# Bias tables made on 128 partitions, paddings filled by GpSimd, and lo parts on VectorE in the second block

## The chip, the cores and the metric

The kernel runs on one core of one Trainium2 chip. The metric is the device time of one execution in microseconds, the median of several runs. In the profile the engines are PE (TensorE matmul), PEld (TensorE weight load), DVE (VectorE), ACT (ScalarE), POOL (GpSimd) and SP (SyncE, which only issues DMAs here). L12 is line 12 of the kernel before.

## The reference

Two transformer blocks run one after the other on 512 tokens of width 1024, in float32. The first has a mixing layer, in which one input projection is split over four mixers, and a feed-forward layer:

```python
z = rms_norm(x, norm1_g) @ w_in
z_pool, s_b, s_c, s_h, c_a, c_g, zq, zk, zv = jnp.split(z, idx, axis=-1)
y_pool = pool_mixer(z_pool, pool_w, pool_scale)          # running sums over 2, 4, 8, 16 tokens
y_sconv = s_b * causal_dwconv(s_c * s_h, sconv_w)        # 3 taps
u = causal_dwconv(c_a * jax.nn.sigmoid(c_g), conf_dw_w) + conf_dw_b   # 31 taps
y_conf = jax.nn.silu(layer_norm(u, conf_ln_g, conf_ln_b))
y_attn = diff_attention(q, k, v, ..., rel_bias)
x = x + jnp.concatenate([y_pool, y_sconv, y_conf, y_attn], axis=-1) @ w_out
x = x + (jax.nn.silu(h2 @ w_gate) * (h2 @ w_up)) @ w_down
```

Both the attention here and the one in the second block add a bias that depends only on the distance of query and key (`rel_bias[rel_bucket(dist)]`, 32 buckets, 4 and 8 heads). The second block prepends 16 meta tokens, so that 528 positions count. Its first half (`layer_ab`) is an attention over the 128 best keys of each query, which an indexer scores and a top-k selects, beside a gated linear attention; its second half (`layer_cd`) is a retention beside a stick-breaking attention.

## The kernel before

**Matrix products.** Activations lie with the features on the partitions. Each float32 factor is split into a hi part (rounded) and a lo part (the rest), and each product is three TensorE products: hi by hi, hi by lo, lo by hi (`f_acc`, L144; `t_proj`, L163). Weights come in blocks of 128 x 1024 values. For each block `weights` issues one load on SP's queue into `wraw` (two buffers, L119), then for each half ScalarE makes the hi part (`whi`, L129) and the engine `self.lo` makes the lo part (`wlo`, L130), with four buffers each. `self.lo` is VectorE, but in `layer_ab` it is GpSimd until the top-k selection is through, and VectorE again from there.

**Order.** Each engine works through its queue in order. A compiler puts the queues together ahead of the run, by priorities: `self.chain()` stands highest, `self.first()` (weights and evictions) next, and the rest by its place in the code. It places an instruction where it reckons that its inputs and its tile's memory are there.

**Setup.** `tables` makes the two bias tables, L378 and L382: a product of the bias (32 buckets by heads) with a one-hot matrix (32 by 640 and by 656 columns). The result lies on 4 and on 8 partitions. VectorE brings it to SBUF (L379, which adds the mask row for future keys, and L383). Two DMAs on GpSimd's queue (L384, L385) write it to DRAM with 32 copies of each row, so that `sheared` (L393) can load each partition with its own shift. The meta tokens' eight loads follow (L387). The tiles of this step lie in a pool of their own, `setup`, which ends with the function.

**First block, mixing layer (`layer1`).** The pool `l1` is opened after `setup`, and part of it lies on the same memory. Its tiles are made in the order qT, kT, cs, B1 (the first table, loaded by GpSimd's queue), pw, u. The projections run in the order cg, ca (`fproj`, evicted at L418), then v, k, q by token (`t_proj`), then z, sc, sh, sb. u = ca * sigmoid(cg) is formed at L446 with 30 columns of zeros ahead (L437). The convolution over 31 taps is 2 x 31 operations of VectorE on u (L560, L562), of normal priority. Attention runs in the background, some steps of it after each few products (`logits` L492 to L503, `turn`, `values` L522, `finish`). The pooling sums (L579, L591, L592) read z with 16 columns of zeros ahead (L567); GpSimd subtracts (L593) and TensorE multiplies with pw (L604). The short convolution reads sc with two columns of zeros ahead (L572), with GpSimd's products at L594 and L600. `mix` splits each mixer's output in hi and lo (L102, L103). The output projection comes in two parts: `add_out(mixed[:4])` for pooling and short convolution, then `add_out(mixed[4:])` for the long convolution, once it is normalised (L613 to L632), and attention.

**Second block, first half (`layer_ab`).** The indexer's scores are products into two PSUM banks, then ScalarE's Relu (L817) and VectorE's weighted sum (L814, L818). The top-k is 16 rounds of VectorE's MAX8 (L827) and MATCH_REPLACE8 (L828) for each of four query tiles. During it TensorE makes the next projections, whose weights come through L129 and L130.

Of the kernel before, what the change touches and what calls it, by code (L numbers as in the profile page):

```python
# [8 lines left out]
F32 = mybir.dt.float32  # L9
# [4 lines left out]
OP = mybir.AluOpType  # L14
# [4 lines left out]
S = 512  # L19
# [5 lines left out]
NEG = -1e30  # L25
# [7 lines left out]
COPIES = 32  # L33
# [20 lines left out]
N1 = 640  # L54
N2 = 656


class Kern:
# [303 lines left out]
    def tables(self):  # L362

        nc, io = self.nc, self.io
        self.tab1 = self.dram.tile([4, COPIES, N1], F32, name="tab1")
        self.tab2 = self.dram.tile([8, COPIES, N2], F32, name="tab2")
        with self.tc.tile_pool(name="setup", bufs=1) as p:
            oh = p.tile([32, N1 + N2], F32, name="oh")
            nc.sync.dma_start(oh, io["onehot"])
            mrow = p.tile([4, N1], F32, name="mrow")  # L370
            nc.sync.dma_start(mrow, io["mrow"])
            rb = p.tile([32, 12], F32, name="relb")
            nc.sync.dma_start(rb, io["relb"])
            t1 = p.tile([4, N1], F32, name="t1")
            t2 = p.tile([8, N2], F32, name="t2")
            for c0, c1 in ((0, 512), (512, N1)):
                ps = self.ch("a")
                nc.tensor.matmul(ps[:4, :c1 - c0], lhsT=rb[:, 0:4], rhs=oh[:, c0:c1], start=True, stop=True)  # L378
                nc.vector.tensor_tensor(out=t1[:, c0:c1], in0=ps[:4, :c1 - c0], in1=mrow[:, c0:c1], op=OP.add)  # L379
            for c0, c1 in ((0, 512), (512, N2)):  # L380
                ps = self.ch("a")
                nc.tensor.matmul(ps[:8, :c1 - c0], lhsT=rb[:, 4:12], rhs=oh[:, N1 + c0:N1 + c1], start=True, stop=True)  # L382
                nc.vector.tensor_copy(t2[:, c0:c1], ps[:8, :c1 - c0])  # L383
            nc.gpsimd.dma_start(self.tab1, t1[:, None, :].to_broadcast([4, COPIES, N1]))  # L384
            nc.gpsimd.dma_start(self.tab2, t2[:, None, :].to_broadcast([8, COPIES, N2]))  # L385
            for k in range(KT):
                nc.gpsimd.dma_start(self.x[k][:, 0:M], io["meta"][k])  # L387

# [7 lines left out]
    def layer1(self):  # L396
        nc, tc = self.nc, self.tc
# [6 lines left out]
        rc, rb = self.norm(acc, False)  # L404
        rbx = rb[:, M:T]
        self.tables()
        with tc.tile_pool(name="l1", bufs=1, reuse_waits="tile") as p:
# [4 lines left out]
            def fproj(out):  # L412
                for f in range(2):
                    w = self.weights(8, 128)
                    ps = self.mm()
                    self.f_acc([ps], w, 0, 128, act, X)
                    with self.first():
                        nc.vector.tensor_tensor(out=out[:, f], in0=ps, in1=rbx, op=OP.mult)  # L418


            qT, kT = (p.tile([128, 8, S], F32R, name=n) for n in ("qT", "kT"))
            cs = p.tile([128, NCS1], F32, name="cs1")
            nc.gpsimd.dma_start(cs, self.io["cs1"])
            B1 = p.tile([128, 4, S], F32, name="B1")
# [7 lines left out]
            lam, gq, gs = self.lam, self.gq, self.gs  # L432


            PADC = 30
            u = p.tile([128, 2, PADC + S], F32, name="u")
            nc.vector.memset(u[:, :, :PADC], 0.0)  # L437
            ca, cg = X2(S), X2(S)
            fproj(cg)
            with self.chain():  # L440
# [3 lines left out]
            with self.chain():  # L444
                for f in range(2):
                    nc.vector.tensor_tensor(out=u[:, f, PADC:], in0=ca[:, f], in1=cg[:, f], op=OP.mult)  # L446

# [116 lines left out]

            PADP = 16
            z = G(PADP + S, "z", "ktok")
            nc.vector.memset(z[:, :, :PADP], 0.0)  # L567
# [4 lines left out]
            nc.vector.memset(sc[:, :, :PADS], 0.0)  # L572
            fproj(sc[:, :, PADS:])
            fproj(sh)
            fproj(sb)
# [26 lines left out]
            for f in range(2):  # L602
                ps = self.ch("b")
# [6 lines left out]
            with self.chain():  # L610
                ps = self.ch("b")
# [6 lines left out]
                ps = self.ch("b")  # L618
# [5 lines left out]
                ps = self.ch("b")  # L624
# [149 lines left out]
    def layer_ab(self, act, acc):  # L774
        nc, tc = self.nc, self.tc
        rc, rb = self.norm(acc, True)
        self.nqk = 12
        self.lo = nc.gpsimd
        with tc.tile_pool(name="ab", bufs=1, reuse_waits="tile") as p:
            F4 = lambda n, w=T: p.tile([128, 4, w], F32, name=n)  # L780
            gw2 = p.tile([128, 256], F32, name="gw2")[64:80]
# [13 lines left out]
            with self.chain():  # L795
                ps = self.ch("b")
# [108 lines left out]
            out = [None] * 8  # L905
# [478 lines left out]
def _constants():  # L1384
    f = np.float32
    p = np.arange(128)
    cst = np.zeros((128, NCST), f)
# [9 lines left out]
    cs1 = np.zeros((128, NCS1), f)  # L1397
# [3 lines left out]
    csa = np.zeros((128, NCSA), f)  # L1401
    start = np.ones(T)
# [3 lines left out]
    csc = np.zeros((128, NCSC), f)  # L1406
# [14 lines left out]
    mrow = np.broadcast_to(np.where(127 + 384 - np.arange(N1) < 0, f(NEG), f(0)), (4, N1))  # L1421
    return {"cst": cst, "cs1": cs1, "csa": csa, "csc": csc, "rot": rot, "onehot": oh, "mrow": np.ascontiguousarray(mrow)}


def _arrays(a):
# [108 lines left out]
```

## Time and profile before

| | us |
|---|---|
| median of 3 runs | 1275.37 (1274.11 to 1275.43) |
| the profiled execution, its own time | 1271.46 |
| its span, first to last instruction | 1269.5 |
| PE, DVE, ACT, POOL busy | 1211.9, 816.2, 615.3, 83.0 |
| mean granted TensorE clock | 0.979 |

The profile shows one execution. A row of the timeline reads: start, length, engine, line, operation, written tile <- read tiles, shapes, how many in a row, and in brackets how long the engine stood idle before it and what ended the wait. A row of a group gives the count, then the busy time and the mean in ns of one, then the idle time before them. A row of the chain of waits gives start, length, engine or DMA, tile, line and count. A row of DMA issues gives the count, the size of one and the median time from issue to landing. The lengths of TensorE's rows overlap each other, as products are pipelined; their starts tell the pace.

### The profile page before, as it was taken

How to read it: one execution, taken by the hardware profiler on the slowest of the kernel's cores; microseconds unless marked ns; L12 is line 12 of the kernel's file. 1: busy time of each engine (PE TensorE's matmuls, PEld its weight loads, DVE VectorE, ACT ScalarE, POOL GpSimd, SP SyncE). 2: the span in 40 equal slices, each digit the busy share in tenths (PEclk: the TensorE clock that was granted, in tenths of full speed). 3: DMA queues.
4: the chain of work that ended last, by engine and by line, in shares of the span. 5: the costliest groups of instructions: out<-in, count | busy, mean ns of one | idle time of the engine just before them, and what ended most of it. 6: DMA issues, size and time to landing. Idle time of an engine off the chain costs nothing.

```text
span 1269.5 us, 19013 instructions
## 1 busy us (share of the span) xinstructions
PE 1211.9 (95%) x7242; PEld 1024.0 (81%) x7242; DVE 816.2 (64%) x1863; ACT 615.3 (48%) x1367; POOL 83.0 (7%) x80
## 2 busy tenths in 40 slices
PE   8599958999999999999999999999999999999997
PEld 5597736888888888888888889899899989886776
DVE  6179997644443444444489989766666476685675
ACT  5167633633322333344444435665555484565654
POOL 2100010200000000002432000000011000000000
PEclk9799979999999999999999999999999999999998
DMA  6722112232223322223311212222213213221121
GB/s 180 107 87 68 34 50 66 84 100 93 90 81 102 116 86 98 90 87 107 109 56 54 73 36 82 68 68 68 82 57 124 84 58 96 72 68 33 50 67 67
DMA packets 33427, 101.44 MB, mean 80 GB/s; under 512 B 4468, under 2 KB 7124, under 8 KB 33336
## 3 DMA queue, kind: packets, MB, share of 16 engines
q1 hardware_dynamic: 30248, 95.87, 23.8%
q0 software_dynamic: 1280, 2.20, 1.7%
q10 hardware_dynamic: 1808, 2.16, 0.5%
q8 instruction: 57, 0.93, 0.3%
q14 instruction: 34, 0.28, 0.1%
HBM read 96.03 MB, written 3.10 MB: 78 GB/s over the span
## 4 chain that ended last, share of the span: by engine, by line
PE 83%; DVE 10%; ACT 3%; DMA 3%; issue 1%; POOL 0%; SPq 0%; DVEq 0%; ACTq 0%; POOLq 0%
PE mm L144 66%; PE psb L174 3%; DMA wraw<-in_w 3%; PE mm L163 2%; DVE sc L818 2%; PE pso L1219 1%; DVE sc L828 1%; DVE m L827 1%; DVE y L562 1%; PE pso L972 1%; DVE wlo L130 1%; PE psa L1100 1%; PE pso L974 1%; ACT whi L129 1%; PE psa L1193 1%
## 5 line engine op out<-in xcount | busy, mean ns | idle before, releaser
L144 PE MATMUL mm<-hhi,whi 128*128 128x512 f32 (+3 forms) x1296 | 443.1, 342 | 3.0 <-ACT whi L129 2.8
L144 PE MATMUL mm<-hhi,wlo 128*128 128x512 f32 (+3 forms) x1296 | 437.3, 337 | 0.2
L144 PE MATMUL mm<-hlo,whi 128*128 128x512 f32 (+3 forms) x1296 | 434.7, 335 | 0.0
L129 ACT CAST whi<-wraw 128x512 fp32r<-128x512 f32 x350 | 207.2, 594 | 352.8 <-PE mm L144 290.6
L130 DVE TENSOR_TENSOR wlo<-wraw,whi 128x512 fp32r<-128x512 f32 x324 | 217.4, 674 | 173.8 <-ACT whi L129 147.8
L144 PEld LDWEIGHTS mm<-hhi,whi 128*128 128x128 f32 (+1 forms) x1296 | 245.1, 189 | 30.6 <-ACT whi L129 3.5
L144 PEld LDWEIGHTS mm<-hhi,wlo 128*128 128x128 f32 (+1 forms) x1296 | 244.6, 189 | 25.8 <-DVE wlo L130 1.0
L144 PEld LDWEIGHTS mm<-hlo,whi 128*128 128x128 f32 (+1 forms) x1296 | 244.7, 189 | 24.9 <-DVE hlo L217 0.7
L144 PE MATMUL mm<-mx,whi 128*128 128x512 f32 (+2 forms) x448 | 114.1, 343 | 3.7 <-ACT mx L102 2.7
L144 PEld LDWEIGHTS mm<-mx,whi 128*128 128x128 f32 x448 | 76.5, 191 | 17.3 <-issue 3.6
L664 DVE TENSOR_TENSOR gu<-mm,rb 128x512 f32<-128x512 f32 x44 | 30.4, 692 | 71.2 <-PE mm L144 69.4
L144 PE MATMUL mm<-mx,wlo 128*128 128x512 f32 (+2 forms) x224 | 75.1, 336 | 0.0
L144 PE MATMUL mm<-hidh,whi 128*128 128x512 f32 x176 | 68.5, 389 | 0.0
L144 PE MATMUL mm<-hidh,wlo 128*128 128x512 f32 x176 | 68.5, 389 | 0.0
L144 PE MATMUL mm<-hidl,whi 128*128 128x512 f32 x176 | 68.5, 389 | 0.0
L231 POOL TENSOR_TENSOR acc<-acc,sq 128x528 f32<-128x528 f32 (+1 forms) x18 | 25.7, 1430 | 623.8 <-PE mm L144 321.7
L300 DVE TENSOR_TENSOR tmp<-mm,rb 128x272 f32<-128x272 f32 (+2 forms) x76 | 35.7, 470 | 29.3 <-PE mm L144 28.1
L562 DVE SCALAR_TENSOR_TENSOR y<-u,cols,y 128x512 f32<-128x512 f32 x60 | 46.4, 781 | 0.4
L288 DVE TENSOR_TENSOR x<-x,mm 128x272 f32<-128x272 f32 (+2 forms) x72 | 36.7, 510 | 14.4 <-PE mm L144 13.2
L144 PEld LDWEIGHTS mm<-mx,wlo 128*128 128x128 f32 x224 | 42.4, 189 | 4.0 <-issue 0.2
L163 PE MATMUL mm<-whi,hhi 128*128 128x256 f32 x96 | 28.5, 297 | 13.7 <-ACT whi L129 12.8
L144 PEld LDWEIGHTS mm<-hidh,wlo 128*128 128x128 f32 x176 | 33.0, 188 | 7.0
(400 smaller groups left out, 1847.3 us busy)
## 6 DMA issues: line engine op xcount, KB each, us to landing
wraw<-in_w SPq DMA_DIRECT2D x145, 512.0 KB, 3.5
wraw<-in_w SPq DMA_DIRECT2D x16, 384.0 KB, 2.9
wraw<-in_w SPq DMA_DIRECT2D x16, 320.0 KB, 2.9
bh<-tab SPq DMA_DIRECT2D x16, 132.0 KB, 2.7
mx<-cqk SPq DMA_DIRECT2D x8, 132.0 KB, 2.4
x<-in_x SPq DMA_DIRECT2D x4, 256.0 KB, 7.2
x<-in_x ACTq DMA_DIRECT2D x4, 256.0 KB, 6.2
B<-tab POOLq DMA_DIRECT2D x4, 256.0 KB, 9.4
```

The lines of the kernel that those rows point to most:

```text
L129: self.nc.scalar.copy(hi[:, :w], raw[:, c])
L130: self.lo.tensor_tensor(out=lo[:, :w], in0=raw[:, c], in1=hi[:, :w].bitcast(F32), op=OP.subtract)
L144: nc.tensor.matmul(ps[b], lhsT=ww[i][:, f0:f0 + nf], rhs=aa[:, t0:t1], start=first and i == 0 and j == 0, stop=last and i == n - 1 and j == 2)
L163: nc.tensor.matmul(part(t), lhsT=aa[:, t0:t0 + nt], rhs=ww[i], start=u + i + j == 0 and t % 2 == 0, stop=u == 1 and i == 3 and j == 2, ski ...
L174: self.nc.tensor.transpose(out, in_, self.ident[:n, :n])
L231: e.tensor_tensor(out=acc[:, c0:c1], in0=acc[:, c0:c1], in1=sq[:, c0:c1], op=OP.add)
L288: nc.vector.tensor_tensor(out=x, in0=x, in1=p, op=OP.add)
L300: self.nc.vector.tensor_tensor(out=out[:, t0:t1], in0=p, in1=rb[:nf, t0:t1], op=OP.mult)
L562: nc.vector.scalar_tensor_tensor(y[:, f], u[:, f, k:k + S], cw[:, f, k:k + 1], y[:, f], op0=OP.mult, op1=OP.add)
L664: nc.vector.tensor_tensor(out=t[:, g], in0=ps, in1=rbx, op=OP.mult)
L818: nc.vector.scalar_tensor_tensor(o, rl, w, o, op0=OP.mult, op1=OP.add)
L827: nc.vector.max(out=m8, in_=sc)
```

## The change

Three things are changed.

The tables are made on 128 partitions. The bias is first copied 32 times by GpSimd (`rbx`), so that the product has 4 heads x 32 copies as its rows; the second table is made in two halves of four heads. A 33rd row of the one-hot matrix holds the mask, with a row of ones in the bias, so that the mask comes out of the product and its own load falls away. VectorE brings the first table to SBUF and ScalarE the two halves of the second, and three DMAs on GpSimd's queue write 128 rows each.

The zero columns ahead of u, z and sc are filled by GpSimd instead of VectorE, and the tile u is made ahead of cs, B1 and pw.

In `layer_ab`, VectorE makes the lo parts of the weights from the start.

```diff
-            oh = p.tile([32, N1 + N2], F32, name="oh")
+            oh = p.tile([33, N1 + N2], F32, name="oh")
             nc.sync.dma_start(oh, io["onehot"])
-            mrow = p.tile([4, N1], F32, name="mrow")
-            nc.sync.dma_start(mrow, io["mrow"])
-            rb = p.tile([32, 12], F32, name="relb")
-            nc.sync.dma_start(rb, io["relb"])
-            t1 = p.tile([4, N1], F32, name="t1")
-            t2 = p.tile([8, N2], F32, name="t2")
-            for c0, c1 in ((0, 512), (512, N1)):
-                ps = self.ch("a")
-                nc.tensor.matmul(ps[:4, :c1 - c0], lhsT=rb[:, 0:4], rhs=oh[:, c0:c1], start=True, stop=True)
-                nc.vector.tensor_tensor(out=t1[:, c0:c1], in0=ps[:4, :c1 - c0], in1=mrow[:, c0:c1], op=OP.add)
-            for c0, c1 in ((0, 512), (512, N2)):
-                ps = self.ch("a")
-                nc.tensor.matmul(ps[:8, :c1 - c0], lhsT=rb[:, 4:12], rhs=oh[:, N1 + c0:N1 + c1], start=True, stop=True)
-                nc.vector.tensor_copy(t2[:, c0:c1], ps[:8, :c1 - c0])
-            nc.gpsimd.dma_start(self.tab1, t1[:, None, :].to_broadcast([4, COPIES, N1]))
-            nc.gpsimd.dma_start(self.tab2, t2[:, None, :].to_broadcast([8, COPIES, N2]))
+            rb = p.tile([33, 12], F32, name="relb")
+            nc.gpsimd.memset(rb[32:33], 1.0)
+            nc.sync.dma_start(rb[:32], io["relb"])
+            rbx = p.tile([33, 12, COPIES], F32, name="rbx")
+            nc.gpsimd.tensor_copy(rbx, rb[:, :, None].to_broadcast([33, 12, COPIES]))
+
+            for h0, c0, n, tab in ((0, 0, N1, self.tab1), (4, N1, N2, self.tab2[0:4]), (8, N1, N2, self.tab2[4:8])):
+                t = p.tile([128, n], F32, name=f"t{h0}")
+                for k0, k1 in ((0, 512), (512, n)):
+                    ps = self.ch("a")[:, :k1 - k0]
+                    nc.tensor.matmul(ps, lhsT=rbx[:, h0:h0 + 4].rearrange("p h c -> p (h c)"), rhs=oh[:, c0 + k0:c0 + k1], start=True, stop=True)
+                    (nc.vector.tensor_copy if h0 == 0 else nc.scalar.copy)(t[:, k0:k1], ps)
+                nc.gpsimd.dma_start(tab.rearrange("h c n -> (h c) n"), t)
...
             qT, kT = (p.tile([128, 8, S], F32R, name=n) for n in ("qT", "kT"))
+            PADC = 30
+            u = p.tile([128, 2, PADC + S], F32, name="u")
+            nc.gpsimd.memset(u[:, :, :PADC], 0.0)
...
-            PADC = 30
-            u = p.tile([128, 2, PADC + S], F32, name="u")
-            nc.vector.memset(u[:, :, :PADC], 0.0)
...
-            nc.vector.memset(z[:, :, :PADP], 0.0)
+            nc.gpsimd.memset(z[:, :, :PADP], 0.0)
...
-            nc.vector.memset(sc[:, :, :PADS], 0.0)
+            nc.gpsimd.memset(sc[:, :, :PADS], 0.0)
...
         rc, rb = self.norm(acc, True)
         self.nqk = 12
-        self.lo = nc.gpsimd
+        self.lo = nc.vector
```

The host's constants change with it: the mask row is joined to the one-hot matrix as its 33rd row.

More of the change, by code (lines that the diff above doesn't have):

```diff
@@ L1420, in _constants @@
     oh[_bucket2(), N1 + np.arange(N2)] = 1
-    mrow = np.broadcast_to(np.where(127 + 384 - np.arange(N1) < 0, f(NEG), f(0)), (4, N1))
-    return {"cst": cst, "cs1": cs1, "csa": csa, "csc": csc, "rot": rot, "onehot": oh, "mrow": np.ascontiguousarray(mrow)}
+    mrow = np.where(np.arange(N1 + N2) < N1, np.where(127 + 384 - np.arange(N1 + N2) < 0, f(NEG), f(0)), f(0))
+    oh = np.concatenate([oh, mrow[None]], 0).astype(f)
+    return {"cst": cst, "cs1": cs1, "csa": csa, "csc": csc, "rot": rot, "onehot": oh}
 def _arrays(a):
```

## The prediction

> **What bounds the kernel now.** I read the span first, then the granted clock and busy time by stretch, then TensorE's gaps in the timeline, then the chain of waits behind each gap, and last the DMA issues.
>
> ```profile
> span 1269.5 us, 19013 instructions
> ```
>
> ```profile
> 20.00:44.20 24.20, 24.20 (x129) 18.61 (x129) 10.34 (x26) 8.86 (x18) 1.98 (x3) 1.00 0.57 71
> 44.20:57.10 12.90, 0.10 (x1) 0.00 (x0) 0.01 (x1) 0.66 (x2) 4.38 (x9) 0.59 0.63 94
> 57.00:200.00 143.00, 125.14 (x718) 103.55 (x718) 129.82 (x329) 79.01 (x213) 8.45 (x6) 0.92 0.23 65
> 57.00:217.00 160.00, 138.84 (x784) 113.71 (x784) 140.93 (x353) 87.28 (x232) 11.40 (x8) 0.93 0.22 65
> 80.00:200.00 120.00, 103.19 (x562) 82.02 (x560) 116.46 (x298) 69.61 (x189) 8.13 (x5) 0.93 0.18 57
> 166.00:188.60 22.60, 9.93 (x27) 4.65 (x27) 22.26 (x34) 8.05 (x13) 4.23 (x3) 0.62 0.15 47
> 640.00:700.00 60.00, 54.86 (x401) 51.93 (x402) 55.68 (x165) 25.36 (x57) 15.76 (x12) 0.97 0.19 62
> ```
>
> Columns: stretch, length, then busy time of PE, PEld, DVE, ACT and POOL, then granted clock, DMA share, GB/s. Over the whole run TensorE is the bound, but not in three stretches: from 44 to 57 every engine stands still; from 80 to 200 VectorE has 116.46 of 120; around 640 to 700 VectorE has 55.68 of 60. The change touches all three. TensorE's gaps:
>
> ```profile
> 38.50 0.28 PE L163 MATMUL mm<-whi,hhi 128*128 128x256 f32 x1
> ...
> 57.11 0.58 PE L163 MATMUL mm<-whi,hhi 128*128 128x256 f32 x1 [12.82 <-ACT whi L129]
> ```
>
> ```profile
> 167.48 1.10 PE L522 MATMUL pso<-vtok,pT 128*128 128x64 f32 x8 [0.68 <-ACT pT L512]
> 180.11 4.20 PE L604 MATMUL psb<-z,pw 128*128 128x512 f32 x4 [11.53 <-POOL z L593]
> 188.58 0.49 PE L144 MATMUL mm<-mx,whi 128*128 128x512 f32 x1 [0.15 <-DVE mx L103]
> ...
> 216.93 0.57 PE L144 MATMUL mm<-mx,whi 128*128 128x512 f32 x1 [0.62 <-DVE mx L103]
> ```
>
> The first gap, in the chain of waits and in the DMA issues:
>
> ```profile
> 21.57 1.17 PE psa L378 x4
> ...
> 31.29 25.07 DMA wraw<-in_w
> ...
> 57.11 14.63 PE mm L163 x96
> ...
> 72.66 8.71 PE mm L163 x72
> ```
>
> ```profile
> wraw<-in_w SPq DMA_DIRECT2D x145, 512.0 KB, 3.5
> B<-tab POOLq DMA_DIRECT2D x4, 256.0 KB, 9.4
> out<-x ACTq DMA_DIRECT2D x4, 256.0 KB, 2.7
> tab<-t POOLq DMA_DIRECT2D x1, 656.0 KB, 25.7
> tab<-t POOLq DMA_DIRECT2D x1, 320.0 KB, 25.6
> ```
>
> A weight block that otherwise lands in 3.5 us took 25.07, exactly while the two table writes were in flight (25.6 and 25.7). They read only 4 and 8 partitions and move 976 KB in 25.7 us, 38 GB/s; the stores of the result, from 128 partitions, move 256 KB in 2.7, 95 GB/s. So the table writes hold the DMA engines, TensorE starves, and its clock falls (0.59).
>
> VectorE, before and in the second stretch:
>
> ```profile
> 33.80 0.06 DVE L572 MEMSET mx<- 128x4 f32 x1
> ...
> 57.09 0.69 DVE L130 TENSOR_TENSOR wlo<-wraw,whi 128x512 fp32r<-128x512 f32 x1 [22.52 <-ACT whi L129]
> 57.70 0.68 DVE L418 TENSOR_TENSOR mx<-mm,rb 128x512 f32<-128x512 f32 x1
> ...
> 68.83 1.29 DVE L446 TENSOR_TENSOR u<-mx 128x512 f32<-128x512 f32 x2
> 70.08 0.11 DVE L437 MEMSET u<- 128x60 f32 x1
> ```
>
> ```profile
> 110.29 0.69 DVE L418 TENSOR_TENSOR z<-mm,rb 128x512 f32<-128x512 f32 x1
> ...
> 172.04 0.09 DVE L567 MEMSET z<- 128x32 f32 x1
> ...
> 172.79 1.25 DVE L579 TENSOR_TENSOR s<-z 128x1054 f32<-128x1054 f32 x1
> ```
>
> ```profile
> L562 DVE SCALAR_TENSOR_TENSOR y<-u,cols,y 128x512 f32<-128x512 f32 x60 | 46.4, 781 | 0.4
> ```
>
> VectorE idles 22.52 us while 46.4 us of convolution (L562) lie ahead, because its queue is in order and u is formed at 68.83. Nothing that u needs is that late: its last input is the eviction at 57.70, queued behind a wlo. And the pooling sums (L579) start at 172.79, though z was complete at 110.98: they stood behind a fill of 0.09 us (L567), ordered behind the convolution. The pooling then feeds L593 on GpSimd and L604, and TensorE waits 11.53 us for it.
>
> **The change, part by part. Table writes.** The three new writes leave 128 partitions with 328, 336 and 336 KB. From the rows, 1000 KB at the stores' 95 GB/s is 10.5 us; the bounds are 2.7 (all three side by side, one store's time) and 26 (as slow as before). I take 10: nearest is the store, with the same direction and the same partitions. They start near 27 to 30, so they are gone by about 40. The table load B, released by the first write, now runs in the thirties; in the trace it took 9.4 a piece. The weight block issued at 31.29 is wanted by TensorE at 44.2 and needs two casts and a lo part first, 2 x 0.59 + 0.67 = 1.9 (rows further down): it may take 11 us where it usually takes 3.5. So I cost the contention at nothing; without that cover each microsecond of lateness is one of stall. Gain on TensorE: 12.82, and the 96 products behind it at the pace of the 72 later ones, 14.63 - 96 x 8.71/72 = 3.0.
>
> Making the tables costs a third product of 656 columns: one table takes 1.17 on TensorE (L378), so +1.2, on the path, since TensorE has no gap from 23 to 44. Four evictions go to ScalarE, which is idle for some microseconds there; VectorE loses two. rbx is a new GpSimd copy that waits for the relb load; behind it in that queue stand only the table writes, which need it, and loads that were issued long before. It has 384 elements a partition, bounded by half and twice the 0.69 of a 512-element VectorE operation, 0.35 to 1.4; I take 0.7, of which TensorE sees at most the excess over one microsecond. One load (mrow) leaves SP's queue. TensorE then stands at its old 71.7 at 71.7 - 12.8 - 3.0 + 1.2 = 57.1, **14.6 earlier**.
>
> **Paddings.** u's tile is now made ahead of cs and B1 and filled by GpSimd. The fill had nothing to wait for, yet stood at 70.08, while sc's fill, much later in the code but in another pool, ran at 33.80. I infer that the order was made as if the pool of u opened only when the setup tiles had been written out, and with short writes that is soon. Then u follows ca's eviction: TensorE ends that product at 38.50, +1.2, so VectorE gets work from 39.7 instead of 57. z's fill leaves VectorE's order: GpSimd does it as soon as ktok is free; behind it on GpSimd wait only sc's fill and the pooling's and short convolution's products (L593, L594, L600), for which VectorE and TensorE wait, and which need later evictions anyway. So the pooling sums run after z's eviction, near 96, and the 11.53 of stall goes.
>
> What is late next is VectorE's work. From 57 to 200 it has 129.82. Started at 39.7, with the idle share of 80 to 200 (3.54 of 120), the convolution ends at 39.7 + 129.82 x 1.03 = 173.4 instead of 200.05; the normalisation behind it took 216.93 - 200.05 = 16.9, so the second output product starts at 190.3 instead of 216.93: **-26.6**. Two bounds beside it: all of VectorE's work to 217 (140.93 x 1.03 from 39.7) is done at 184.9, -32; TensorE alone is ready at 168.58 - 14.6 + 2.1 (L604 at full clock) + 25.0 (188.58 to 216.93 without its waits of 3.3) = 181.1, **-36**. I take -26.6, as the convolution fills VectorE's gaps and so tends to end last. From 217 on TensorE is busy without a gap, and the gain stays:
>
> ```profile
> 217.00:245.00 28.00, 28.00 (x118) 22.64 (x119) 21.20 (x31) 16.96 (x30) 8.81 (x6) 0.94 0.29 94
> ```
>
> **Lo parts.**
>
> ```profile
> L130 POOL TENSOR_TENSOR wlo<-wraw,whi 128x512 fp32r<-128x512 f32 (+1 forms) x26 | 33.5, 1289 | 59.9 <-ACT whi L129 55.9 <-ACT rb L257 3.8
> L130 DVE TENSOR_TENSOR wlo<-wraw,whi 128x512 fp32r<-128x512 f32 x324 | 217.4, 674 | 173.8 <-ACT whi L129 147.8
> ```
>
> ```profile
> L129 ACT CAST whi<-wraw 128x512 fp32r<-128x512 f32 x350 | 207.2, 594 | 352.8 <-PE mm L144 290.6
> ```
>
> ```profile
> L818 DVE SCALAR_TENSOR_TENSOR sc<-rl,iw,sc 128x272 f32<-128x272 f32 x14 | 9.2, 657 | 0.1
> L814 DVE TENSOR_SCALAR sc<-psa,iw 128x272 f32<-128x272 f32 x2 | 1.0, 489 | 0.0
> ```
>
> ```profile
> 607.72 1.79 DVE L231 TENSOR_TENSOR acc<-acc,sq 128x528 f32<-128x528 f32 x1
> ```
>
> Twenty-six go from GpSimd to VectorE at 0.67. Fourteen lie before 640 under VectorE's slack there and cost nothing (up to 9 if that were gone). Twelve lie from 640 to 700, on the bounding engine: +8.1. Against it, VectorE's two-input operation L818 takes 657 where the one-input L814 on the same elements takes 489: 0.168 over 35 of them is 5.9, more on the wider ones, and goes when GpSimd is quiet. Bounds -2 and +8; I take +1.5, and -1 for the sum of squares at 607.72, whose 1.79 is stretched likewise (0.7 is usual for its size). Together 0.
>
> The Trainium skill (SBUF — State Buffer, Who interferes with whom) has GpSimd and VectorE exclude each other for a whole instruction. By that rule the twelve would give back their full 1.29 each, 15.5, and the sum would be about 8 lower; the trace shows 5.9, so I keep the row.
>
> **Sum.** 1271.5 (the profiled execution, span 1269.5 and 2.0 around it) - 26.6 + 0.5 = 1245. The runs' median is 1275.4, 3.9 above that execution; on their scale 1275.4 - 27 = **1248**.
>
> **Rivals.** *TensorE is the next bound* (-36): the convolution is through before the attention's busy stretch, 1240. For it: VectorE stands still for 12.9 us from 44. Against: the normalisation's chain of 16.9. *u stays late*: if the order still puts u behind four more wlo, it follows the second product after 44, at 38.5 + 1.2 + 2 x 5.8 + 2 = 53, 16 before 68.83; gain 16, **1259**. For it: the order before; against: the fill's place. *The writes stay slow or B takes their part*: the weights land as late, the convolution still ends as before; only TensorE's later stall shrinks, which VectorE covers: 0 to -3, **1274**. For it: B's 9.4; against: the stores' 2.7. The Trainium skill (SBUF — State Buffer, Door 1: The DMA port swizzle) ties a DMA's rate to the ports its partitions reach; by it tab1 and half of tab2, 648 KB at 27.2 GB/s, would take an estimated 24.4, and the trace's 25.7 agrees.
>
> *Slower*: VectorE waits at the head of its queue for the casts. GpSimd waited 55.9 us for whi before 20 of its lo parts, 2.8 each. If all twelve on the bounding stretch waited so, 12 x 2.8 + 1.5 = +35; it decides once it exceeds the 27, from 2.1 a piece, and at the full price gives **1283**. Against: VectorE already makes lo parts in the same helper after 700 without waits. *The port frees more*: if each lo part had blocked VectorE for its whole 1.29, the stretch gives 12 x (1.29 - 0.67) = 7.4, and with it 1241. The rule quoted above says this; the rows do not.
>
> **How the numbers follow.** Forecast 1248: 55. TensorE-bound 1240: 13. u late 1259: 18. Port 1241: 3. Writes slow 1274: 7. Slower 1283: 4. The range 1239 to 1262 holds all but the last two and the tails. I call 0.2%, 2.5 us, what a measurement can tell. Of "writes slow" about half is within it. Faster 0.92, same 0.04, slower 0.04.
>
> **What would show it.** Right: weight blocks near 31 landing within 11 us; no gap at 44; clock 1.00 there; u near 41 and convolution in the forties; L579 before 110; the second output product near 190. Wrong: u behind the wlo at 53; a gap left at 44 with B in flight; VectorE idle before L130 with ScalarE as releaser between 640 and 700.

## The result, and the profile after

| kernel | median of its runs, us | range | profiled execution | span | clock |
|---|---|---|---|---|---|
| before | 1274.74 (4 runs) | 1271.99 to 1275.43 | 1271.46 | 1269.5 | 0.979 |
| after | 1237.56 (4 runs) | 1234.41 to 1241.89 | 1235.71 | 1233.9 | 0.992 |

The ratio is 0.9715, with a 95% interval from 0.9678 to 0.9751: 32 to 41 us came off, 35.6 by the two spans. The forecast was 1248, its range 1239 to 1262: the direction was right, and the gain was larger than the range allowed. One run of a later kernel, the one with more products on TensorE, took 2336.77 us where its three others took 1238 to 1240, and is left out of its median.

The stretches that the prediction read, in the changed kernel (columns as there):

```profile
20.00:44.20 24.20, 23.83 (x103) 17.63 (x104) 13.82 (x30) 10.48 (x22) 7.21 (x16) 0.93 0.47 137
44.20:57.10 12.90, 12.90 (x112) 12.90 (x112) 12.90 (x21) 4.06 (x8) 0.00 (x0) 1.00 0.34 116
39.00:169.80 130.80, 127.61 (x782) 107.96 (x780) 126.99 (x326) 80.18 (x213) 8.28 (x6) 1.00 0.22 71
```

Where every engine stood still, TensorE and VectorE now both have 12.90 of 12.90 at full clock. Its DMA issues, first those from 24 to 60 us, then the table writes:

```profile
wraw<-in_w SPq DMA_DIRECT2D x5, 512.0 KB, 4.0
...
B<-tab POOLq DMA_DIRECT2D x4, 256.0 KB, 5.3
...
tab<-t POOLq DMA_DIRECT2D x2, 328.0 KB, 2.8
...
tab<-t POOLq DMA_DIRECT2D x1, 320.0 KB, 2.4
```

The table writes take 2.4 to 2.8 us where they took 25.7, and the weight blocks land in 4.0. VectorE in the first block, and the last pieces of its convolution:

```profile
37.65 0.69 DVE L444 TENSOR_TENSOR u<-mx 128x512 f32<-128x512 f32 x1
38.44 0.55 DVE L558 TENSOR_SCALAR y<-u,cols 128x512 f32<-128x512 f32 x1
39.02 0.75 DVE L560 SCALAR_TENSOR_TENSOR y<-u,cols,y 128x512 f32<-128x512 f32 x1
...
95.86 1.24 DVE L577 TENSOR_TENSOR s<-z 128x1054 f32<-128x1054 f32 x1
...
168.21 1.53 DVE L560 SCALAR_TENSOR_TENSOR y<-u,cols,y 128x512 f32<-128x512 f32 x2
```

Two of TensorE's waits, the one for the tables and the one behind the convolution, and the first product after the first block (L246):

```profile
20.37 1.34 PE L381 MATMUL psa<-oh,rbx 33*128 33x512 f32 x4 [1.45 <-POOL rbx L375]
...
184.46 2.38 PE L144 MATMUL mm<-mx,whi 128*128 128x512 f32 x4 [2.89 <-ACT mx L102]
...
578.45 1.16 PE L246 MATMUL pso<-ones,acc 128*128 128x1 f32 x10
```

The same marks before: VectorE's time up to the first tap of the convolution and from there on, then the first tap, the last tap and L246.

```profile
57.00:70.20 13.20, 13.09 (x85) 12.87 (x86) 5.76 (x10) 3.24 (x7) 0.32 (x1) 0.75 0.72 142
70.20:200.10 129.90, 112.16 (x636) 90.69 (x634) 124.11 (x319) 75.77 (x206) 8.13 (x5) 0.93 0.18 57
```

```profile
70.22 0.55 DVE L560 TENSOR_SCALAR y<-u,cols 128x512 f32<-128x512 f32 x1
...
199.30 0.75 DVE L562 SCALAR_TENSOR_TENSOR y<-u,cols,y 128x512 f32<-128x512 f32 x1
...
609.65 1.16 PE L246 MATMUL pso<-ones,acc 128*128 128x1 f32 x10 [0.94 <-DVE acc L231]
```

Read them together. From the first tap to the end of the last it takes 129.8 us before and 131.3 after, and VectorE is 96 and 97% busy there (TensorE 86 and 98%). The convolution ends 30.3 earlier (200.05, now 169.74), because it begins 31.8 earlier (70.22, now 38.44), and L246 comes 31.2 earlier. That is the first block's gain. The second block's first half gives the other 4.4 of the 35.6. Its scoring stage, from the first score product to the first product of what follows (L1018, now L1016), is 639.1 to 684.3 before and 607.7 to 646.3 after; VectorE's and GpSimd's groups before, to 684.0 (so that both sides hold 32 of the scoring operations), then VectorE's after:

```profile
L818 DVE SCALAR_TENSOR_TENSOR sc<-rl,iw,sc 128x272 f32<-128x272 f32 (+3 forms) x32 | 21.9, 686 | 2.4 <-ACT rl L817 2.0
L827 DVE MAX8 m<-sc 128x8 f32<-128x144 f32 (+1 forms) x23 | 7.9, 344 | 0.3
L828 DVE MATCH_REPLACE8 sc<-m,sc 128x144 f32<-128x144 f32 (+1 forms) x23 | 7.6, 330 | 0.0
...
L130 POOL TENSOR_TENSOR wlo<-wraw,whi 128x512 fp32r<-128x512 f32 x9 | 11.9, 1322 | 33.8 <-ACT whi L129 33.8
```

```profile
L816 DVE SCALAR_TENSOR_TENSOR sc<-rl,iw,sc 128x272 f32<-128x272 f32 (+3 forms) x32 | 15.6, 490 | 1.2 <-ACT rl L815 0.9
L130 DVE TENSOR_TENSOR wlo<-wraw,whi 128x512 fp32r<-128x512 f32 x9 | 6.2, 683 | 0.7 <-ACT whi L129 0.6
L825 DVE MAX8 m<-sc 128x8 f32<-128x144 f32 (+1 forms) x18 | 5.8, 322 | 0.2
L826 DVE MATCH_REPLACE8 sc<-m,sc 128x144 f32<-128x144 f32 (+1 forms) x18 | 5.5, 308 | 0.0
```

Nine lo parts cost VectorE 6.2, and 32 two-input scoring operations give back 6.3 (21.9 to 15.6). VectorE pays nothing for its new work, yet the stage is 6.6 shorter (45.2, now 38.6). Five of its 23 rounds of the top-k now stand behind the stage, and TensorE's waits are gone: these are all of them, before (after there is none), and the two stages with TensorE's busy time first and its clock behind the five engines.

```profile
PE psa L809 <- DVE sc L814: 3.8, 3, 2.1
PE psa L810 <- DVE qk L703: 0.5, 1, 0.5
```

```profile
639.10:684.30 45.20, 40.85 (x306) 39.63 (x304) 41.60 (x123) 18.22 (x44) 11.58 (x9) 0.96 0.18 59
```

```profile
607.70:646.30 38.60, 38.60 (x306) 37.90 (x304) 35.66 (x115) 18.24 (x44) 0.00 (x0) 1.00 0.23 69
```

4.3 of the 6.6 are the waits; most of the rest goes with the clock, which was 0.96 beside them and is 1.00.

### The profile page after: what moved, and what is told of

It reads as the page before. It is cut to its first block, busy times and chain, and to the rows that moved or that the text cites. A ratio compares the mean times of both kernels' runs of the same rounds, so it can differ in the third digit from the quotient of the medians.

```text
span 1233.9 us, 19017 instructions
## 1 busy us (share of the span) xinstructions
PE 1208.5 (98%) x7246; PEld 1022.3 (83%) x7246; DVE 819.1 (66%) x1884; ACT 617.1 (50%) x1371; POOL 51.0 (4%) x60
## 3 DMA queue, kind: packets, MB, share of 16 engines
q1 hardware_dynamic: 30236, 95.86, 24.4%
## 4 chain that ended last, share of the span: by engine, by line
PE 87%; DVE 8%; ACT 2%; DMA 1%; issue 1%; POOL 0%; SPq 0%; DVEq 0%; POOLq 0%
PE mm L144 70%; PE psb L174 3%; DVE y L560 2%; DVE wlo L130 1%; PE pso L1217 1%; PE pso L970 1%; DVE sc L826 1%; PE psa L1098 1%; DVE m L825 1%; PE pso L972 1%; PE psa L1191 1%; DMA wraw<-in_w 1%; PE mm L163 1%; DMA relb<-in_relb 1%; PE psb L1191 0%
## 5 line engine op out<-in xcount | busy, mean ns | idle before, releaser
L130 DVE TENSOR_TENSOR wlo<-wraw,whi 128x512 fp32r<-128x512 f32 x350 | 235.0, 674 | 156.3 <-ACT whi L129 128.8
L144 PEld LDWEIGHTS mm<-hlo,whi 128*128 128x128 f32 (+1 forms) x1296 | 245.1, 189 | 26.6 <-issue 1.6
L144 PEld LDWEIGHTS mm<-mx,whi 128*128 128x128 f32 x448 | 76.7, 192 | 15.6 <-ACT mx L102 3.7
L144 PEld LDWEIGHTS mm<-hidh,whi 128*128 128x128 f32 x176 | 33.0, 188 | 6.9
```

What stands on the lines that cost most here:

```text
L130: self.lo.tensor_tensor(out=lo[:, :w], in0=raw[:, c], in1=hi[:, :w].bitcast(F32), op=OP.subtract)
L144: nc.tensor.matmul(ps[b], lhsT=ww[i][:, f0:f0 + nf], rhs=aa[:, t0:t1], start=first and i == 0 and j == 0, stop=last and i == n - 1 and j == 2)
```

## The experiments

Times are medians. "The changed kernel" is the 1237.56 above; it ran once more beside the copy on GpSimd and two of the versions meant to be faster (1236.49), and these are compared with that. The last product alone, and the tables with the lo parts, ran in another group without it. L246 stands for the first product after the first block in every kernel. Line numbers shift by a few from kernel to kernel.

**The parts one by one.** Tables alone, paddings alone, lo parts alone, and the changed kernel without one part. The edits are the hunks of the change, taken or left; the lo part is one line:

```
-        self.lo = nc.gpsimd
+        self.lo = nc.vector
```

Tables alone:

> The tables alone: three products from 128 partitions, rbx, the wide writes; the paddings' fills stay on VectorE and the lo parts of the second block's first half on GpSimd. Theory (the late weights and TensorE's own work set the first block; u and z came late because the order was made with slow table writes): no gap at 44, u near 40, the pooling sums near 100, the second output product near 185, and about 31 us off in all (near 1243). Rival (u's place and z's fill on GpSimd are needed for it): only the stall at 44 goes, u stays behind the weights, L604 still waits some 11 us, 15 us off at most (near 1260).

Paddings alone:

> The paddings alone: u made earlier, the fills of u, z and sc by GpSimd; the narrow table writes stay. The weights still land late and TensorE still stands still for some 13 us at 44, with u behind lo parts that wait for these weights. Theory (TensorE's work sets the end of the first block once z is free): the 11.5 us before L604 go and with them some small waits, 11 to 17 us off (1258 to 1264). Rival (VectorE's convolution sets it, from 57 on as before): its 129.82 us of work to 200 with 3 per cent of idle time end near 191, 9 us off at most; or nothing at all, if VectorE's order has the pooling as late as before (1266 to 1275).

Lo parts alone:

> The lo parts alone, moved to VectorE in the second block's first half. Theory (GpSimd's lo parts stretch VectorE's two-input operations beside them by 0.17 to 0.28 us, and slow GpSimd ones keep weights waiting): about 4 us off (near 1271), L818 at 490 ns for 128x272 against 657. Rival (12 lo parts on the bounding stretch cost VectorE as much as the quiet gives back): no change within 1 us.

Tables and paddings, without the lo parts:

> The changed kernel with the lo parts left on GpSimd in the second block's first half: tables and paddings. Theory: about 31.5 us off, as the first block's gain alone (near 1243), and 4 us more than the changed kernel's time; the scoring operation takes 657 ns for 128x272 again. Rival (the lo parts do nothing, the two parts of the first block make the whole gain): 35 to 37 us off, near 1238.

Tables and lo parts, without the paddings:

> The changed kernel without the paddings' part: the fills of u, z and sc stay on VectorE and u's tile is made where it was before; tables and lo parts as changed. Theory (with wide writes u and the pooling are early anyway): u near 40 against 37.65, so 2 us above the changed kernel (near 1239), 1 to 4. Rival (z's fill on GpSimd takes away 11.5 us of TensorE's waiting by itself): 8 or more above.

| kernel | median, us | ratio to before, 95% | span | u formed | last tap ends |
|---|---|---|---|---|---|
| tables | 1248.27 | 0.9798 [0.9764, 0.9832] | 1244.8 | 39.82 | 172.7 |
| paddings | 1278.68 | 1.0032 [1.0021, 1.0044] | 1275.0 | 66.72 | 202.4 |
| lo parts | 1263.75 | 0.9922 [0.9902, 0.9943] | 1261.7 | 66.77 | 197.8 |
| tables, paddings | 1245.38 | 0.9769 [0.9744, 0.9794] | 1239.2 | 37.88 | 170.5 |
| tables, lo parts | 1240.71 | 0.9749 [0.9725, 0.9773] | 1237.9 | 38.42 | 174.3 |

The tables alone make u early, with its fill still on VectorE and its tile where it was: the theory's mechanism holds. Its size is 21 to 30 us, a little short of the 31 expected; at L246 it is 27.9 (609.65, now 581.71). Before, four lo parts stand in VectorE's queue between the eviction at 57.70 and u, and the last two wait 6.59 for their weights; with the tables alone one lo part stands between. With the paddings alone u stays at 66.72, although the code puts its tile ahead of cs and B1. So the place of u came from the tables, by the order in VectorE's queue, not from the paddings. Why the compiler orders them so is inferred; no run shows it. The paddings alone missed both expectations: they lost time. TensorE's waits at the end of the first block in that run, with the pooling sums and the last taps of VectorE ahead of them:

```profile
109.64 1.24 DVE L579 TENSOR_TENSOR s<-z 128x1054 f32<-128x1054 f32 x1
...
197.68 4.68 DVE L562 SCALAR_TENSOR_TENSOR y<-u,cols,y 128x512 f32<-128x512 f32 x6
```

```profile
202.42 2.08 PE L613 MATMUL psb<-y,m 128*128 128x512 f32 x2 [5.98 <-DVE y L562]
205.94 3.74 PE L621 MATMUL psb<-ones,ysq 128*128 128x1 f32 x16 [1.44 <-ACT ysq L617]
211.00 1.11 PE L207 MATMUL psb<-keep,yr 128*128 128x128 f32 x4 [1.32 <-DVE yr L203]
218.69 0.79 PE L144 MATMUL mm<-mx,whi 128*128 128x512 f32 x1 [5.93 <-ACT mx L102]
```

The pooling sums come at 109.64 instead of 172.79 and the 11.53 us before L604 are gone, but the waits are only elsewhere: 5.98, 1.44, 1.32 and 5.93. VectorE has as much to do as before and ends at 202.4; TensorE has spent the products that used to lie beside the normalisation, and stands bare there. On top of the tables the paddings take another 4.0 us off by the spans (1237.9 with tables and lo parts, 1233.9 with all three) and 5.6 without the lo parts; at L246 it is 4.2 and 2.2. The intervals of the runs overlap or touch, so the size is known to a few us only. The tables with the lo parts came as expected, 3.2 above the changed kernel (1 to 4).

The lo parts alone are worth 9.9 us by the ratio (7 to 13), 7.8 by the span, of which 2.2 were there when the last tap ended, before any lo part had moved; about 4 had been expected. On top of the other two parts they are worth 5.3 by the span. Counted from L246 to the end it is 6.1 alone and 4.3 on top. The scoring stage shows it most plainly: it is 45.1 to 45.2 us long before, with the paddings alone and without the lo parts, 43.6 with the tables alone, and in these kernels TensorE waits 3.7 to 3.8 there for the scoring operation. With the lo parts moved it is 38.6, alone or with the others, and that wait is gone.

**Who sets the end of the first block.** Three edits of the changed kernel: the convolution held back, 6 us more on VectorE, and more products on TensorE.

```
-            nc.gpsimd.memset(u[:, :, :PADC], 0.0)
...
+                if not b:
+                    for f in range(2):
+                        nc.gpsimd.tensor_scalar(u[:, f, :PADC], vt[:, 3, :PADC], 0.0, None, op0=OP.mult)
```

> The changed kernel, with u's padding written as zero times the last token tile of v, so that the convolution can't begin before v's eviction, near 54.5 instead of 38.4; nothing else is moved, the weights land as early. Theory (from u on, VectorE's 130 us of work set the end of the first block): the convolution ends 16 us later less the lo parts and sums that VectorE does meanwhile, some 3, so 13 us above the changed kernel (near 1251), with TensorE waiting for VectorE later on. Rival (TensorE's own work sets it, 127.6 of 130.8 us busy there): its spare 3.2 us take the delay, 0 to 5 us above.

```
+                for _ in range(12 if f == 0 else 1):
+                    nc.vector.tensor_scalar(y[:, f], u[:, f, 0:S], cw[:, f, 0:1], cb[:, f:f + 1], op0=OP.mult, op1=OP.add)
```

> The changed kernel, with the first operation of the convolution (0.55 us) done 12 times instead of once for the first half: 6 us more on VectorE in the first block, nothing more on TensorE. Theory (VectorE's work sets the end of the first block): 6 us above the changed kernel, 5 to 7. Rival (TensorE's work sets it, VectorE has 4 of 131 us spare): 0 to 2 above.

```
+        for _ in range(extra):
+            nc.tensor.matmul(ps[0], lhsT=w[0][0][:, f0:f0 + nf], rhs=act[0][0][:, toks[0][0]:toks[0][1]], start=True, stop=True)
...
-            fproj(z[:, :, PADP:])
+            fproj(z[:, :, PADP:], 7)
```

> The changed kernel, with 14 more TensorE products of 512 columns (0.43 us each) in the projection of z, written where the first product of the same sum overwrites them: 6 us more on TensorE in the first block, nothing more on VectorE. Theory (VectorE's work sets the end; TensorE has 3.2 us of idle time in 130.8): 3 us above the changed kernel, 1 to 4. Rival (TensorE sets it): 6 above. If both this and the run with more VectorE work lose the full 6, the two engines wait for each other in turn.

The convolution held back: 1260.98, 23.4 above the changed kernel, ratio 0.9903 [0.9886, 0.9919]. The table writes are quick and no weight is late in it, and still two thirds of the gain are lost: TensorE's stall at 44 was not what the 31 us were made of. L246 comes at 603.79, 25.3 of the 31.2 lost. The loss is larger than the 13 expected. VectorE's first tap, and TensorE's wait for the last one:

```profile
56.14 1.00 DVE L560 TENSOR_SCALAR y<-u,cols 128x512 f32<-128x512 f32 x2 [0.46 <-POOL u L550]
```

```profile
192.93 2.07 PE L613 MATMUL psb<-y,m 128*128 128x512 f32 x2 [7.55 <-DVE y L562]
```

The first tap comes 17.7 later than at 38.44, the last tap ends 23.1 later, at 192.9. The 3 us that I subtracted for work done meanwhile did not come back: from 56.1 to 192.9 VectorE is 7.9 us idle (128.89 of 136.80), where the changed kernel has 3.8 of 130.8. The likely reason, not tested, is that taps are also what VectorE does between other waits.

Six us more on VectorE: 1244.41, 6.9 above by the medians, 9.1 by the spans. More products on TensorE: 1239.38, 1.8 above by the medians, 3.6 by the spans. That test was weaker than meant: the 14 products run one behind the other and took 3.8 us (1.78 + 1.09 + 0.95), not 6. L246 with more work on VectorE, then on TensorE, against 578.45:

```profile
589.15 1.16 PE L246 MATMUL pso<-ones,acc 128*128 128x1 f32 x10
```

```profile
583.62 1.16 PE L248 MATMUL pso<-ones,acc 128*128 128x1 f32 x10
```

By the medians the theory that VectorE sets the end held, and by this mark it did not hold alone. VectorE's 6 us put L246 off by 10.7, with the last tap 10.6 later (180.29). TensorE's 3.8 put it off by 5.2, although the last tap then ends 2.2 earlier (167.54). By this mark, in one profile of each, both cost more than was added, which is the expectation's third case: the two engines wait for each other in turn, and neither shows slack. What is shown is that the start of the convolution moves the end; that VectorE alone is the bound is not. The order of the queues changes a little with each of these edits, so the sizes are known to a few us only.

**Why the lo parts help.** GpSimd makes the lo part a second time, or copies the raw weights, into a tile that nothing reads. `self.beside` is set from the start of `layer_ab` until the top-k selection is through:

```
+                if self.beside:
+                    self.nc.gpsimd.tensor_tensor(out=self.g[:, :w], in0=raw[:, c], in1=hi[:, :w].bitcast(F32), op=OP.subtract)
```

> The changed kernel, with GpSimd making every lo part of the second block's first half a second time, into a scratch tile that nothing reads, beside the one that VectorE makes. No lo part comes later by it. Theory (GpSimd's two-input operations stretch VectorE's beside them): the scoring operation is back from 491 towards 657 ns for 128x272, and 5 to 7 us of the gain between the first and the last scoring product go, so near 1243. Rival (the gain came from lo parts that are ready sooner, 0.68 us against 1.29, with weights waiting less): no loss above 1.5 us, the scoring operation keeps 491 ns.

```
+                if self.beside:
+                    self.nc.gpsimd.tensor_copy(self.g[:, :w], raw[:, c])
```

> The changed kernel, with a GpSimd copy (one input) of every raw weight half of the second block's first half into a scratch tile, where the run with the two-input operation made the lo part a second time (1253, 15 above). Theory (it is GpSimd's second input beside VectorE's two-input operations that stretches them): 0 to 3 above the changed kernel, the scoring operation at 491 to 520 ns for 128x272, VectorE's lo parts near 684. Rival (any GpSimd operation of this length beside VectorE does it): 10 to 15 above, 650 ns and more.

With the second lo part 1253.11, 15.5 above the changed kernel, ratio 0.9843 [0.9826, 0.986]; with the copy 1236.80, 0.3 above. VectorE's two kinds of two-input work and GpSimd's own in the scoring stage, with the second lo part, then with the copy:

```profile
L820 DVE SCALAR_TENSOR_TENSOR sc<-rl,iw,sc 128x272 f32<-128x272 f32 (+3 forms) x31 | 21.8, 706 | 1.7 <-ACT rl L819 1.4
L130 DVE TENSOR_TENSOR wlo<-wraw,whi 128x512 fp32r<-128x512 f32 x8 | 7.1, 888 | 0.6 <-ACT whi L129 0.6
...
L132 POOL TENSOR_TENSOR g<-wraw,whi 128x512 f32<-128x512 f32 x10 | 14.3, 1429 | 33.6 <-issue 31.6 <-ACT whi L129 1.7
```

```profile
L820 DVE SCALAR_TENSOR_TENSOR sc<-rl,iw,sc 128x272 f32<-128x272 f32 (+3 forms) x32 | 16.9, 531 | 0.9 <-ACT rl L819 0.6
L130 DVE TENSOR_TENSOR wlo<-wraw,whi 128x512 fp32r<-128x512 f32 x9 | 6.2, 684 | 0.7 <-ACT whi L129 0.6
...
L132 POOL COPY g<-wraw 128x512 f32<-128x512 f32 x10 | 6.8, 683 | 33.1 <-DMA wraw<-in_w 32.8
```

With the second lo part VectorE's own take 888 ns instead of 683, still less than GpSimd's 1322 before, and TensorE waits in the stage for the scoring operation (4.6 us) and never for a lo part. So the rival (lo parts that are ready sooner) falls, and GpSimd's operation beside VectorE's is shown as the cause. The size per us of GpSimd's work in this stage: before, 6.3 us lost by VectorE on 11.9 of GpSimd, 0.53. With the second lo part 31 x (706 - 490) ns + 8 x (888 - 683) ns = 8.3 on 14.3, 0.58. With the copy 32 x (531 - 490) ns = 1.3 on 6.8, 0.19. The copy is half as long and takes less per us too; whether its single input or its length does that, this pair of runs cannot tell.

These means hide how it happens. Single operations of VectorE in the kernel before, then one of GpSimd's lo parts:

```profile
662.17 0.62 DVE L818 SCALAR_TENSOR_TENSOR sc<-rl,iw,sc 128x400 f32<-128x400 f32 x1
...
663.11 0.31 DVE L827 MAX8 m<-sc 128x8 f32<-128x144 f32 x1
663.33 1.56 DVE L818 SCALAR_TENSOR_TENSOR sc<-rl,iw,sc 128x400 f32<-128x400 f32 x1
```

```profile
663.17 1.29 POOL L130 TENSOR_TENSOR wlo<-wraw,whi 128x512 fp32r<-128x512 f32 x1 [7.07 <-ACT whi L129]
```

The scoring operation that starts 0.16 us after the lo part takes 1.56 instead of 0.62 and ends 0.43 after it; MAX8, which reads one tile, keeps its 0.31. At eight of the nine lo parts of this stage the first scoring operation that starts inside is stretched by 0.3 to 1.0 us; the ninth starts just behind a scoring operation (683.02) and is itself stretched, to 1.59. Operations that meet no lo part keep their time, so the mean of 686 ns is a mixture. A copy does it too, for less: beside the copies at 628.09 a scoring operation of the 0.62 kind took 1.04.

The Trainium skill (SBUF — State Buffer, Who interferes with whom) says that a VectorE instruction with two inputs in SBUF contends with a GpSimd instruction that reads SBUF, and calls the ports that they share an exclusive lock. Operation by operation the trace agrees: the 1.56 us above are the rest of the lo part, 1.13, and 0.43 of the operation's own. The share of 0.5 to 0.6 over the stage is lower, since part of VectorE's work passes untouched.

The second lo part cost 16.6 by the spans; 5 to 7 had been expected, in the scoring stage alone. In the stage it is 8.1 (38.6, with it 46.7), as VectorE's own lo parts are stretched with the scoring; 1.8 lie ahead of L246, 2.3 from there to the stage, and 4.4 behind it, where the operation is also added.

**Versions meant to be faster.** The changed kernel again, then the early loads with the last product on VectorE, then ScalarE for two kinds of one-input operations on top, then the last product alone:

```
-            nc.sync.dma_start(oh, io["onehot"])
+            nc.gpsimd.dma_start(oh, io["onehot"])
...
-            nc.sync.dma_start(rb[:32], io["relb"])
+            nc.gpsimd.dma_start(rb[:32], io["relb"])
...
-                    nc.gpsimd.tensor_tensor(out=y[:, f], in0=y[:, f], in1=ysq[:, f], op=OP.mult)
+                    nc.vector.tensor_tensor(out=y[:, f], in0=y[:, f], in1=ysq[:, f], op=OP.mult)
```

> The changed kernel itself, beside the three others of this call: 1236 to 1239.

> A version meant to be faster: the one-hot table and relb are loaded by GpSimd's queue at the start instead of SP's near 12.5, and the last product of the normalisation (y<-y,ysq) is made by VectorE instead of GpSimd. Theory: TensorE's wait of 1.45 us for rbx goes, u is formed 1.5 earlier, and since VectorE sets the end of the first block, that and a GpSimd operation of 1.49 that becomes 0.7 take 2 us off the changed kernel (near 1235). Rival (the early load of 167 KB delays the first weights and x): no gain, or up to 2 lost.

```
-                nc.vector.tensor_scalar(y[:, f], u[:, f, 0:S], cw[:, f, 0:1], cb[:, f:f + 1], op0=OP.mult, op1=OP.add)
+                nc.scalar.activation(y[:, f], u[:, f, 0:S], AF.Identity, bias=cb[:, f:f + 1], scale=cw[:, f, 0:1])
...
-                    nc.vector.tensor_scalar(sh[:, f], sc[:, f, 0:S], sw[:, f, 0:1], None, op0=OP.mult)
+                    nc.scalar.mul(sh[:, f], sc[:, f, 0:S], sw[:, f, 0:1])
```

> The version with the early loads, and in addition ScalarE makes the first, one-input operation of the convolution (2 x 0.55 us) and of the short convolution (2 x 0.55) in place of VectorE. Theory (VectorE sets the end of the first block): another 1.5 to 2.2 off (near 1233). Rival (TensorE sets it, or ScalarE's queue brings these late): no gain over the version with the early loads alone.

> The changed kernel, with only the last product of the normalisation (y<-y,ysq, 2 x 1.49 us) made by VectorE instead of GpSimd; the table inputs are loaded as in the changed kernel. Theory (the 5 us that the version with early loads won came from the serial chain behind the convolution, whose wait of 2.89 us before the second output products was gone there): 3 to 5 us off the changed kernel (1232 to 1234), and no wait of TensorE above 1 us before these products. Rival (they came from the early loads and the wait of 1.45 us for rbx): no gain within 1.5 us.

| kernel | median, us | range | ratio to before, 95% |
|---|---|---|---|
| the changed kernel again | 1236.49 | 1232.42 to 1240.52 | 0.971 [0.9687, 0.9734] |
| early loads, last product | 1231.50 | 1229.0 to 1232.38 | 0.9668 [0.9649, 0.9686] |
| and ScalarE's operations | 1237.98 | 1233.12 to 1238.88 | 0.9714 [0.9692, 0.9736] |
| last product alone | 1235.59 | 1230.22 to 1239.44 | 0.9679 [0.9657, 0.9702] |

The version with early loads is the fastest of all that ran by its median, 5 us below the changed kernel beside it, the intervals only just apart. The reason that I gave for half of it is wrong. Its u is formed at 38.63, later than 37.65: the wait for rbx was not saved, it stands at 8.60 and is 3.33 long. What is shorter is the way from the last tap to L246, in this version and in the one with the last product alone:

```profile
167.89 1.53 DVE L560 SCALAR_TENSOR_TENSOR y<-u,cols,y 128x512 f32<-128x512 f32 x2
...
575.80 1.16 PE L246 MATMUL pso<-ones,acc 128*128 128x1 f32 x10
```

```profile
176.29 1.54 DVE L560 SCALAR_TENSOR_TENSOR y<-u,cols,y 128x512 f32<-128x512 f32 x2
...
583.53 1.16 PE L246 MATMUL pso<-ones,acc 128*128 128x1 f32 x10
```

From the end of the last tap it is 406.4 and 405.7 us, against 408.7 in the changed kernel. That the last product on VectorE gives these 2 to 3 us is not shown: the version with ScalarE's operations holds the same edit and has 408.7 (172.60 to 581.34). In the run with that product alone the wait before the second output products is still 2.45 us, where the theory said none above 1; most of its 3.0 come behind that wait, with TensorE's clock at 1.00 from 173 to 221 where the changed kernel has 0.93 from 165 to 213. Its median is 0.9 below the changed kernel's, by the ratios to before 4, as it ran in another group, in a range of 9 us: neither theory's number is clearly reached.

ScalarE's operations gave nothing; the taps at 41.41 in that version wait for ScalarE (0.34). By the medians they lost 6.5, the intervals apart (0.9692 to 0.9736, 0.9649 to 0.9686); L246 comes 5.5 later than with the early loads alone (581.34, 575.80). Why is open.

## Why the prediction was right, and where it fell short

- **The table writes.** The stall at 44 (12.82) went, and the tables alone make it go. I took 10 us for the writes, between 2.7 and 26; they took 2.4 to 2.8, the lower bound. It changed nothing, since the weights had 11 us to spare. The third product was put at 1.2 and rbx at less than that: L381 is 4.6 us against 2.6 for its two predecessors, and TensorE waited 1.45 for rbx, because relb, issued at 12.97, took 6.33.
- **Paddings.** u near 41 and the sums near 96 came (37.65 and 95.86). That short writes put u early was right, and it was the tables' doing: alone they give 39.82 and 102.49. That the move and the fills are needed for it was not. And "the 11.53 of stall goes" was true of that gap only: the paddings alone took it away and lost 4 us.
- **What is late next.** VectorE, and behind it the normalisation: right in that the convolution held back takes the gain away. That TensorE is ready well before it was wrong: it is 127.61 of 130.80 busy, and more work on it puts off the end as well. So the rival that TensorE is the next bound (1240), nearest in the number, was half right: the two now wait for each other.
- **A step that failed: "the convolution ends at 39.7 + 129.82 x 1.03 = 173.4".** The 129.82 is VectorE's work from 57, but it was made to start at the time of u, and of it 5.76 lie ahead of the first tap at 70.22. From the first tap to the end of the last VectorE has 127.5 of work in the changed kernel (126.99 in the row from 39.00, and the first tap), 2.3 less than I counted, with 3.8 idle as I took it; and the tap starts at 38.44, 1.3 sooner. So the end came at 169.74, 3.7 before 173.4: a term mis-sized, not a wrong path. I also held the second output product to be the one at 216.93, and its twin behind the wait on mx stood at 215.34; in the gain this nearly cancels, as 16.9 stood on both sides (15.3 and 14.7 measured, 0.6 of gain). At the end of the first block it is 31.2 against 26.6: 3.7, 0.6, and 0.3 behind.
- **The other step that failed, lo parts: "Together 0"** (0.5 in the sum), **4.4 off measured** (35.6 - 31.2). The balance of VectorE's work was right almost to the tenth, 6.2 against 6.3. Wrong was to price the stage by VectorE alone: TensorE's wait was put at nothing. TensorE had waited 3.8 us there for the scoring operation; with that operation shorter it no longer does, and rounds of the top-k move behind the stage. At L246, 31.2 had been gained; by the end of the scoring stage it is 38.0 (684.3, now 646.3); at the end 35.6, so 2.4 are given back later.
- **The sum.** On its own execution I had 1245 against the 1235.71 that ran: 9.3 short, 9.7 before rounding: 4.6 from the first block, 4.9 from the lo parts, 0.2 outside the span. My scale, median 3.9 above the execution, held to 2 us (1237.56 against 1235.71).
- **The rivals that fell.** u behind the lo parts at 53; writes that stay slow; VectorE idle before L130 with ScalarE as releaser: 0.6 us of such idle time in the scoring stage. "Port frees more" had the right mechanism. The prediction set it aside by the mean stretch of 0.168 us, which averages a few operations held for up to 1 us with many that were not touched; per us of GpSimd's work about half came.

## What to carry to other kernels

Before a stall is booked as gain, find the engine whose work runs from there to the next meeting point, and measure from the instruction at which that work can begin, not from the end of the stall: here the start of one operation, 32 us earlier, carried the first-block gain, and taking away a wait of 11.53 us on another engine gave nothing while that operation still began late. When an engine gives up as much work as it takes on, look whether the other engine's waits for it change, since the stage may get shorter all the same. And read single operations, not only the mean of a group: a mean of 686 ns hid operations of 0.6 and of 1.6 us. A slow transfer can cost twice, by the stall it makes and by the place to which it pushes other instructions in an order made ahead of time; here the second was the larger.

## What the runs showed of the hardware

Runs of one kernel spread by up to 9 us here (1230 to 1239), and the clock goes with it: in the five runs of the version with the last product on VectorE it is 0.988 in the slowest and 0.995 in the two fastest. A part of that lies near the start. The granted clock (the first column behind the five engines) from 22 to 40 us in the profiled execution of the version with the last product on VectorE, in pieces:

```profile
22.00:24.00 2.00, 2.00 (x5) 1.61 (x6) 0.30 (x1) 0.00 (x0) 0.00 (x0) 0.50 0.00 0
...
30.00:34.00 4.00, 4.00 (x7) 1.57 (x6) 0.00 (x0) 0.87 (x2) 0.55 (x1) 0.50 0.05 17
...
38.00:40.00 2.00, 2.00 (x6) 1.52 (x6) 1.29 (x2) 1.97 (x4) 2.00 (x5) 0.50 0.65 201
```

TensorE is busy in all of each piece and stays at 0.50 for 18 us, behind a wait of 1.45 us at 20.13; in the changed kernel, with the same wait at 20.37, the clock is 0.87 from 26 to 39. u's first half is formed at 45.16 there, 37.65 in the changed kernel, and the last tap ends 8 us later. The Trainium skill (TensorE: Matmul & The Clock Gate, Part 1: The HAM clock gate) has the clock come up after some 3.4 us of busy time; this run shows five times that. A gain of 2 to 3 us in one part of this kernel is therefore not settled by medians of four runs, nor by a mark inside one trace without the clock beside it.
